# Two matmul widths for the split planes of an expert layer, an addition behind them, and two pieces of work placed elsewhere in the order

## The chip, the cores and the metric

The kernel runs on one core of a Trainium2 chip. The metric is the device time of one execution in microseconds (us). TensorE (PE; its weight loads are listed as PEld) does the matmuls, VectorE (DVE) and ScalarE (ACT) work on whole tiles, GpSimd (POOL) does small work and issues the gathers, SyncE (SP) issues the weight loads.

## The reference

The program is two transformer blocks over 256 tokens of width 1024, all in fp32. The change lies in the expert layer at the end of the first block and at the start of the second block. The expert layer is, cut to what matters:

```
q  = (xc @ w_query).reshape(C, 8, 2, 128)             # 8 heads, two halves
sc = einsum('thpd,hpnd->thpn', q, sub_keys)           # scores against 128 keys a half
... top 16 of each half, top 16 of their sums: 8 x 16 experts of 16384 for each token, softmax gates
act = gelu(einsum('cd,chkd->chk', xc, expert_down[experts]))
out = einsum('chk,chkd->cd', gates * act, expert_up[experts])
```

The second block begins with a normalisation and the projections of the normalised rows; it also needs the values of a memory of 256 rows, `mem_n @ w_kv`.

## The kernel before

**Expert layer.** The 16384 experts lie as 128 planes of 128. For the last 192 tokens (`ND = 192`) the kernel does not gather: it multiplies every plane of `expert_down` with all 192 tokens, applies gelu, multiplies with the gates (zero where an expert is not chosen), keeps the products in `slots` [128 x 128 planes x 192 tokens], and then multiplies `slots` with every plane of `expert_up`. For the first 64 tokens (`NS = 64`) it gathers the chosen rows with indirect DMAs: 64 `dot` steps (line 764, POOL fetches 128 rows, DVE multiplies and sums) and 64 `axpy` steps (line 771). These are spread over the planes (`state["k"]`, `KD`, `KU`).

**Down planes (lines 838 to 867).** The loop goes over 64 pairs of planes. One PSUM bank (`mm_tile`, a ring of four banks) takes both planes of a pair, 2 x 192 columns. The first plane of a pair is always "whole": 8 fp32 matmuls against `xf` (`whole_plane`, line 834), each of which the trace lists as two instructions. From plane `JS = 24` on the second plane of a pair is "split": the weights are loaded to `raw`, ACT rounds them to `hi` (line 61), DVE makes `lo = raw - hi` (line 62), and PE multiplies in the fp32r type: for each of 8 k-steps `hi` with `xh`, `hi` with `xl`, `lo` with `xh`, 192 columns each (`gemm_t`, lines 96 to 101). `xh` and `xl` are the two parts of the activations, two separate tiles. Before `JS` the second plane is whole too. After each pair ACT applies gelu (lines 864, 866) and DVE multiplies the tokens whose gates are ready into `slots` (line 867).

The gates of 8 tokens at a time come from `gates_of` (line 799): DVE makes one-hot tables, ACT scales one of them in 8 instructions (line 819), 16 small matmuls place the gates (line 825), DVE or ACT writes them into `slots` (lines 830, 832). 24 such groups are spread over the planes from `J0 = 34` to `J1 = 122`. What they read comes from `turns[t]` (line 742: 4 transposes on PE, copies on ACT, one DVE subtraction), called at planes 14 and 28; the tables they turn come from a long chain of top-16 searches on DVE (lines 674 to 751), which runs beside the first planes.

**Up planes (lines 899 to 927).** For each of 128 planes ACT copies the activations into `a2` (lines 904, 905, kept in program order), DVE makes their low part (line 911), the weights are split as above, and 10 matmuls of 512 columns accumulate into four banks `acc` for the whole loop, which are all four of the `mm` ring. The last three planes are held back and done first for the first 128 tokens, then for the others; DVE adds the sums to `x_sb` (lines 924, 926) and ACT takes their squares.

**Start of the second block (lines 942 to 952).** `mem_values(0)` is a product of 4 weight chunks (48 matmuls of 512 columns, `gemm_n`, line 103) into the two `at` banks. It does not depend on the expert layer. `norm_t` then normalises `x_sb` and `rows_t` transposes it for the projections.

**What sets the order.** The instructions of each engine are put into a fixed order when the program is built, by a planner that simulates the engines: work that is ready comes by its place in the program, `split` comes with a higher priority, and an instruction marked `keep_in_program_order` is not moved past others. At run time each engine works through its list.

Of the kernel before, what the change touches and what calls it, by code (L numbers as in the profile page):

```python
# [9 lines left out]
F32 = mybir.dt.float32  # L10
F32R = mybir.dt.float32r
# [4 lines left out]
OP = mybir.AluOpType  # L16
# [3 lines left out]
P = 128  # L20
T = 256
NT = 2
D = 1024
KT = 8
EPS = 1e-6
NEG = -1e30
CH = 1024
LASTN = 3
NS = 64
ND = T - NS  # L30
# [5 lines left out]
def f32v(ap):  # L36
    return ap.bitcast(F32)
# [3 lines left out]
def layers_kernel(ctx: ExitStack, tc: tile.TileContext, a: dict, out: bass.AP, upto: str = "all"):  # L41
    nc = tc.nc
    V, S, G, PE = nc.vector, nc.scalar, nc.gpsimd, nc.tensor
# [7 lines left out]
    def mm_tile():  # L51
        return psum.tile([P, 512], F32, name="mm", tag="mm", bufs=4)
# [18 lines left out]
    def stream(src, raw=None):  # L71
        if ahead:
            return ahead.pop(0)
        if raw is None:
            raw = stream_p.tile([P, CH], F32, name="raw", tag="raw", bufs=3)
        nc.sync.dma_start(raw, src)
        own = more["at"] % (3 + more["n"]) < 3
        more["at"] += 1
        pool, b = (stream_p, 3) if own else (more["pool"], more["n"])
        hi = pool.tile([P, CH], F32R, name="hi", tag="hi", bufs=b)  # L80
        lo = pool.tile([P, CH], F32R, name="lo", tag="lo", bufs=b)
        with tc.high_priority():
            split(raw, hi, lo)
        return hi, lo
# [11 lines left out]
    def gemm_t(o, xh, xl, w, kts=KT):  # L96
        for k in range(kts):
            hi, lo = w[0][:, k * P:(k + 1) * P], w[1][:, k * P:(k + 1) * P]
            PE.matmul(o, hi, xh[:, k, :], start=(k == 0), stop=False)  # L99
            PE.matmul(o, hi, xl[:, k, :], start=False, stop=False)  # L100
            PE.matmul(o, lo, xh[:, k, :], start=False, stop=(k == kts - 1))  # L101

    def gemm_n(xh, xl, w, s, kts=KT, steps=(), tail=None, bank=mm_tile):


        os = [bank() for _ in range(NT)]
        nch = kts // 2
        last = {nch - 1 - i: None for i in range(LASTN)}

        def mms(kp, w, t):  # L110
            hi, lo = w
            sl = slice(t * P, (t + 1) * P)
            for k2 in range(2):
                k = kp * 2 + k2
                wh, wl = hi[:, k2 * 512:(k2 + 1) * 512], lo[:, k2 * 512:(k2 + 1) * 512]
                PE.matmul(os[t], xh[:, k, sl], wh, start=(k == 0), stop=False)  # L116
                PE.matmul(os[t], xh[:, k, sl], wl, start=False, stop=False)  # L117
                PE.matmul(os[t], xl[:, k, sl], wh, start=False, stop=(k == kts - 1))  # L118

        for kp in range(nch):  # L120
            ws = stream(w[s, kp])
            if tail and kp in last:
                last[kp] = ws
            else:
                for t in range(NT):
                    mms(kp, ws, t)
            if kp < len(steps):
                for f in steps[kp]:
                    f()
        if tail:  # L130
            for t in range(NT):
                for kp in sorted(last):
                    mms(kp, last[kp], t)
                tail(t, os[t])
        return os
# [137 lines left out]
    with ExitStack() as c1:  # L273
        b1 = c1.enter_context(tc.tile_pool(name="b1", bufs=1))
        scr = c1.enter_context(tc.tile_pool(name="b1s", bufs=2))
        xh = b1.tile([P, KT, T], F32R, name="xh", tag="xh")
        xl = b1.tile([P, KT, T], F32R, name="xl", tag="xl")
# [293 lines left out]
    with ExitStack() as c2:  # L571
        pr = c2.enter_context(tc.tile_pool(name="peer", bufs=1))
        prs = c2.enter_context(tc.tile_pool(name="peers", bufs=2))
        xh = fx.tile([P, KT, T], F32R, name="fh")
        xl = fx.tile([P, KT, T], F32R, name="fl")
        xf = pr.tile([P, KT, ND], F32, name="ff", tag="ff")
        slots = pr.tile([P, P, ND], F32, name="slots")
        TG = 8
# [87 lines left out]
        turns = {}  # L666
# [132 lines left out]
        def gates_of(g, j):  # L799
# [20 lines left out]
            for part in range(0, TG, 4):  # L820
# [10 lines left out]
                if j < P:  # L831
                    S.copy(sv[:, j:], gv[:, j:])

        def whole_plane(o, w):
            for k in range(KT):
                PE.matmul(o, w[:, k * P:(k + 1) * P], xf[:, k, :], start=(k == 0), stop=(k == KT - 1))  # L836

        J0 = 34
        J1 = 122
        K0 = 12  # L840
        KD = 76
        JS = 24
        for jp in range(P // 2):
            j = 2 * jp
            if j >= J0:
                while state["g"] < min(NG, G0 - (-(NG - G0) * (j - J0 + 2) // (J1 - J0))):
                    gates_of(state["g"], j)
                    state["g"] += 1
            while state["k"] < KD * (jp - K0 + 1) // (P // 2 - K0):
                step()  # L850
            if j in (14, 28):
                turns[j // 14 - 1]()
            nt = state["g"] * TG - NS
            o = mm_tile()
            for jj in range(2):
                ot, src = o[:, jj * ND:(jj + 1) * ND], a["peer_down"][j + jj]
                if j >= JS and jj == 1:
                    gemm_t(ot, xh[:, :, NS:], xl[:, :, NS:], stream(src))
                else:
                    whole_plane(ot, stream_whole(src))  # L860
            ov = o[:, :2 * ND].rearrange("p (j t) -> p j t", j=2)
            dst = slots[:, j:j + 2, :]
            if nt < ND:
                S.activation(dst[:, :, nt:], ov[:, :, nt:], AF.Gelu)
            if nt > 0:
                S.activation(ov[:, :, :nt], ov[:, :, :nt], AF.Gelu)
                V.tensor_tensor(dst[:, :, :nt], ov[:, :, :nt], dst[:, :, :nt], op=OP.mult)
# [31 lines left out]
        for j in range(P):  # L899
            while state["k"] < min(2 * HALF, KD + -(-(2 * HALF - KD) * (j + 1) // KU)):  # L900
                step()

            a2 = prs.tile([P, 7 * NS], F32R, name="a2", tag="oh1")
            tc.keep_in_program_order(S.copy(a2[:, :ND], slots[:, j, :]))  # L904
            tc.keep_in_program_order(S.copy(a2[:, ND:T], slots[:, j, :NS]))
            raw = None
            if j % 6 > 2:

                raw = pr.tile([P, KT * ND], F32, name="raw_f", tag="ff")[:, :CH] if j % 6 == 4 else                     prs.tile([P, CH], F32, name="raw_o", tag="ohs")
            uh, ul = stream(a["peer_up"][j], raw)  # L910
            V.tensor_tensor(a2[:, T:], slots[:, j, :], f32v(a2[:, :ND]), op=OP.subtract)  # L911
            if j >= P - LASTN:
                held.append((j, (uh, ul, a2)))
            else:
                for t in range(NT):
                    ups(j, (uh, ul, a2), t)
# [22 lines left out]

        return [rows_p.tile([P, KT, T], F32R, name="rows_" + n, tag="rows_" + n) for n in "hl"]  # L940

    def mem_values(s, steps=(), bank=mm_tile):
        os = gemm_n(nh, nl, a["w_xv"], s, steps=steps, bank=bank)
        for t in range(NT):
            S.copy(v_m[:, t, s * 512:(s + 1) * 512], os[t])

    with ExitStack() as c3:
        b2 = c3.enter_context(tc.tile_pool(name="b2", bufs=1))
        scr = c3.enter_context(tc.tile_pool(name="b2s", bufs=1))
        xh, xl = rows_pair()  # L950
        mem_values(0, bank=at_tile)
        norm_t(x_sb, ss_mix, 2, xh, xl, [scr.tile([P, D], F32, name="xs%d" % t, tag="aT", bufs=2) for t in range(NT)])

        cols = load(b2, a["cols"], [P, 40], "cols")
# [433 lines left out]
```

## Time and profile before

| | |
|---|---|
| median of 3 runs | 1457.79 us (1457.25 to 1458.81) |
| profiled execution | 1459.28 us |
| its span, first to last instruction | 1457.2 us |
| PE busy | 1424.1 us (98%) |
| DVE busy | 1032.0 us (71%) |
| ACT busy | 769.4 us (53%) |
| POOL busy | 282.9 us (19%) |
| moved by DMA | 336.95 MB, mean 231 GB/s |

Busy time of PE is the union of its instructions. A matmul's duration in the list is its passage through the array; matmuls overlap, so what one costs in a row of them is the distance from its start to the start of the next. The profiled execution took 1.49 us more than the median, and 2.08 us of it lie outside the span.

### The profile page before, as it was taken

Reading aid. Unit: us, or ns where it says so; the run is one execution under the profiler, and the core shown is the slowest. Engines: PE = TensorE matmul, PEld = TensorE weight load, DVE = VectorE, ACT = ScalarE, POOL = GpSimd, SP = SyncE. Lnnn points to the kernel's source line nnn. Section 1 sums busy time; section 2 is a strip of 40 time slices with the busy share of each in tenths; the row PEclk is TensorE's granted clock in tenths of the full one; section 3 lists DMA queues with packets and bytes.
Section 4 is the critical chain, followed back from the end, with each engine's and each line's share of the span. In section 5 each row is a group of like instructions: output and inputs, shape, how many; then the busy total and the mean of one; then the engine's idle time right before and its main releaser. Section 6 shows DMA issues by size and latency. Waiting matters only on the chain. (4 is left out here: it accounts for less than half of the span.)

```text
span 1457.2 us, 24511 instructions
## 1 busy us (share of the span) xinstructions
PE 1424.1 (98%) x9144; PEld 1274.8 (87%) x9144; DVE 1032.0 (71%) x1841; ACT 769.4 (53%) x1497; POOL 282.9 (19%) x222
## 2 busy tenths in 40 slices
PE   9999999999999999899999999899999999999998
PEld 7778899999999999677777778797999989899886
DVE  7975678968878887688888876464565555566553
ACT  6565552336556552466666665484445455555442
POOL 4721000133332323333333300040101100000000
PEclk9999999999999999999999999999999999999999
DMA  7535557488898888999999976434456564455553
GB/s 270 159 109 178 190 186 238 144 317 315 300 326 314 310 313 327 363 326 324 336 330 332 330 235 213 162 130 130 133 175 196 179 193 144 146 196 189 188 188 114
DMA packets 93703, 336.95 MB, mean 231 GB/s; under 512 B 10736, under 2 KB 12656, under 8 KB 92816
## 3 DMA queue, kind: packets, MB, share of 16 engines
q1 hardware_dynamic: 73376, 259.79, 52.9%
q0 software_dynamic: 19344, 73.41, 14.0%
q10 hardware_dynamic: 864, 2.19, 0.4%
q8 instruction: 72, 1.18, 0.3%
q14 instruction: 47, 0.39, 0.1%
HBM read 331.15 MB, written 4.19 MB: 230 GB/s over the span
## 5 line engine op out<-in xcount | busy, mean ns | idle before, releaser
L62 DVE TENSOR_TENSOR lo<-raw,hi 128x1024 fp32r<-128x1024 f32 x345 | 424.6, 1232 | 263.2 <-ACT hi L61 258.1
L61 ACT CAST hi<-raw 128x1024 fp32r<-128x1024 f32 x345 | 361.7, 1049 | 433.5 <-PE mm L100 163.6
L836 PE MATMUL mm<-ff,whole 128*128 128x192 f32 x1216 | 209.1, 328 | 0.0
L99 PE MATMUL mm<-rows_h,hi 128*128 128x256 f32 x736 | 204.8, 283 | 2.5 <-ACT qT_x L1226 1.1
L100 PE MATMUL mm<-rows_l,hi 128*128 128x256 f32 x736 | 205.9, 281 | 0.7 <-DVE rows_l L199 0.7
L101 PE MATMUL mm<-rows_h,lo 128*128 128x256 f32 x736 | 205.4, 281 | 1.0 <-DVE lo L62 1.0
L836 PEld LDWEIGHTS mm<-ff,whole 128*128 128x128 f32 x1216 | 196.3, 190 | 0.0
L99 PE MATMUL mm<-fh,hi 128*128 128x192 f32 (+1 forms) x544 | 155.4, 289 | 0.7 <-ACT hi L61 0.5
L101 PE MATMUL mm<-fh,lo 128*128 128x192 f32 (+1 forms) x544 | 150.2, 277 | 2.3 <-DVE lo L62 2.3
L100 PE MATMUL mm<-fl,hi 128*128 128x192 f32 (+1 forms) x544 | 151.1, 279 | 0.0
L99 PEld LDWEIGHTS mm<-rows_h,hi 128*128 128x128 f32 x736 | 137.9, 190 | 3.9 <-ACT hi L61 1.4
L100 PEld LDWEIGHTS mm<-rows_l,hi 128*128 128x128 f32 x736 | 139.1, 189 | 1.6 <-DVE rows_l L199 1.0
L101 PEld LDWEIGHTS mm<-rows_h,lo 128*128 128x128 f32 x736 | 139.1, 189 | 1.6 <-DVE lo L62 1.6
L760 POOL DMA_INDIRECT fetched<-in_down_rows,picks x64 | 82.6, 1290 | 287.8 <-DVE fetched L766 152.0
L760 POOL DMA_INDIRECT fetched<-in_peer_up,picks x64 | 98.0, 1531 | 202.0 <-DVE sums L776 183.9
L891 PE MATMUL mm<-hi,a 128*128 128x512 f32 x256 | 101.8, 398 | 6.6 <-DVE a L911 6.6
L101 PEld LDWEIGHTS mm<-fh,lo 128*128 128x128 f32 x544 | 104.6, 192 | 2.5 <-DVE lo L62 2.5
L99 PEld LDWEIGHTS mm<-fh,hi 128*128 128x128 f32 x544 | 103.9, 192 | 1.1 <-ACT hi L61 1.0
L100 PEld LDWEIGHTS mm<-fl,hi 128*128 128x128 f32 x544 | 104.6, 192 | 0.1
L894 PE MATMUL mm<-hi,a 128*128 128x512 f32 x256 | 101.7, 397 | 0.7 <-ACT a L904 0.7
L895 PE MATMUL mm<-lo,a 128*128 128x512 f32 x256 | 101.7, 397 | 0.0
L892 PE MATMUL mm<-lo,a 128*128 128x512 f32 x256 | 101.7, 397 | 0.0
(379 smaller groups left out, 2827.0 us busy)
## 6 DMA issues: line engine op xcount, KB each, us to landing
whole<-in_peer_down SPq DMA_DIRECT2D x76, 512.0 KB, 4.8
raw<-in_peer_up SPq DMA_DIRECT2D x65, 512.0 KB, 6.2
raw<-in_peer_down SPq DMA_DIRECT2D x52, 512.0 KB, 5.7
raw<-in_w_in_2t SPq DMA_DIRECT2D x52, 512.0 KB, 3.5
raw_o<-in_peer_up SPq DMA_DIRECT2D x42, 512.0 KB, 6.2
raw<-in_w_up SPq DMA_DIRECT2D x32, 512.0 KB, 3.6
raw<-in_w_down SPq DMA_DIRECT2D x32, 512.0 KB, 3.5
raw<-in_w_in SPq DMA_DIRECT2D x24, 512.0 KB, 4.4
```

What stands on the lines that cost most here:

```text
L61: S.copy(hi, src)
L62: V.tensor_tensor(lo, src, f32v(hi), op=OP.subtract)
L99: PE.matmul(o, hi, xh[:, k, :], start=(k == 0), stop=False)
L100: PE.matmul(o, hi, xl[:, k, :], start=False, stop=False)
L101: PE.matmul(o, lo, xh[:, k, :], start=False, stop=(k == kts - 1))
L760: G.indirect_dma_start(out=r, out_offset=None, in_=tables[table], in_offset=bass.IndirectOffsetOnAxis(ap=picks[:, k:k + 1], axis=0))
L836: PE.matmul(o, w[:, k * P:(k + 1) * P], xf[:, k, :], start=(k == 0), stop=(k == KT - 1))
L891: PE.matmul(acc[0][hf], both, uh[:, ds], start=first, stop=False)
L892: PE.matmul(acc[0][hf], both, ul[:, ds], start=False, stop=last)
L894: PE.matmul(acc[1][hf], high, uh[:, ds], start=first, stop=False)
L895: PE.matmul(acc[1][hf], high, ul[:, ds], start=False, stop=False)
```

## The change

The two parts of the activations become one tile (`xhl`), so that both stand beside each other for each k-step. A split plane now goes to a bank of its own: for each k-step `hi` is multiplied with 384 columns (high and low part of 192 tokens), `lo` with 192, in 16 instructions for 24; the low half of the result is then copied by ACT to `part` and added by DVE to the high half, into the pair's bank. `JS` goes from 24 to 32, `J0` from 34 to 36, and the turns from planes 14 and 28 to 18 and 32. The `a2` of the first two up planes is made before the last pair of down planes. In the `mem_values(0)` call the first matmul of each token tile is kept in program order. (One long line is also written as four.)

```diff
-    def gemm_n(xh, xl, w, s, kts=KT, steps=(), tail=None, bank=mm_tile):
+    def gemm_n(xh, xl, w, s, kts=KT, steps=(), tail=None, bank=mm_tile, behind=False):
...
-                PE.matmul(os[t], xh[:, k, sl], wh, start=(k == 0), stop=False)
+                m = PE.matmul(os[t], xh[:, k, sl], wh, start=(k == 0), stop=False)
+                if behind and k == 0:
+                    tc.keep_in_program_order(m)
...
-        xh = fx.tile([P, KT, T], F32R, name="fh")
-        xl = fx.tile([P, KT, T], F32R, name="fl")
+        xhl = fx.tile([P, KT, 2, T], F32R, name="fhl")
+        xh, xl = xhl[:, :, 0, :], xhl[:, :, 1, :]
...
+        def split_plane(o, w):
+            o2 = o[:, :2 * ND].rearrange("p (s t) -> p s t", s=2)
+            for k in range(KT):
+                hi, lo = w[0][:, k * P:(k + 1) * P], w[1][:, k * P:(k + 1) * P]
+                if k < KT - 1:
+                    PE.matmul(o2, hi, xhl[:, k, :, NS:], start=(k == 0), stop=False)
+                PE.matmul(o[:, :ND], lo, xh[:, k, NS:], start=False, stop=False)
+                if k == KT - 1:
+                    PE.matmul(o2, hi, xhl[:, k, :, NS:], start=False, stop=True)
...
+        def parts_of(j):
+            a2 = prs.tile([P, 7 * NS], F32R, name="a2", tag="oh1")
+            tc.keep_in_program_order(S.copy(a2[:, :ND], slots[:, j, :]))
+            tc.keep_in_program_order(S.copy(a2[:, ND:T], slots[:, j, :NS]))
+            return a2
+
+        def low_parts(a2, j):
+            V.tensor_tensor(a2[:, T:], slots[:, j, :], f32v(a2[:, :ND]), op=OP.subtract)
+            return a2
+
+        parts = []
-        J0 = 34
+        J0 = 36
...
-        JS = 24
+        JS = 32
...
-            if j in (14, 28):
-                turns[j // 14 - 1]()
+            if j in (18, 32):
+                turns[j // 32]()
+            if jp == P // 2 - 1:
+                parts.extend(low_parts(parts_of(j), j) for j in range(2))
...
                 if j >= JS and jj == 1:
-                    gemm_t(ot, xh[:, :, NS:], xl[:, :, NS:], stream(src))
+                    o1 = mm_tile()
+                    split_plane(o1, stream(src))
+                    part = prs.tile([P, ND], F32, name="part", tag="part")
+                    S.copy(part, o1[:, ND:2 * ND])
+                    V.tensor_tensor(ot, o1[:, :ND], part, op=OP.add)
...
-            a2 = prs.tile([P, 7 * NS], F32R, name="a2", tag="oh1")
-            tc.keep_in_program_order(S.copy(a2[:, :ND], slots[:, j, :]))
-            tc.keep_in_program_order(S.copy(a2[:, ND:T], slots[:, j, :NS]))
+            a2 = parts[j] if j < 2 else parts_of(j)
...
-            V.tensor_tensor(a2[:, T:], slots[:, j, :], f32v(a2[:, :ND]), op=OP.subtract)
+            if j >= 2:
+                low_parts(a2, j)
...
-    def mem_values(s, steps=(), bank=mm_tile):
-        os = gemm_n(nh, nl, a["w_xv"], s, steps=steps, bank=bank)
+    def mem_values(s, steps=(), bank=mm_tile, behind=False):
+        os = gemm_n(nh, nl, a["w_xv"], s, steps=steps, bank=bank, behind=behind)
...
-        mem_values(0, bank=at_tile)
+        mem_values(0, bank=at_tile, behind=True)
```

## Rows read from the trace of the kernel before

**Rows 1.** Windows: stretch, us; busy (x) of PE, PEld, DVE, ACT, POOL; clock, DMA share, GB/s.

```profile
222.00:592.00 370.00, 364.33 (x2864) 362.88 (x2863) 303.29 (x739) 171.14 (x422) 101.09 (x79) 1.00 0.82 292
330.00:540.00 210.00, 210.00 (x1758) 209.65 (x1757) 177.57 (x301) 118.17 (x311) 65.92 (x53) 1.00 0.88 311
510.00:540.00 30.00, 30.00 (x256) 29.91 (x256) 27.41 (x45) 16.50 (x45) 8.24 (x7) 1.00 0.86 296
...
582.00:599.00 17.00, 10.38 (x79) 10.24 (x78) 11.60 (x14) 6.24 (x11) 6.58 (x8) 0.93 0.99 362
...
599.00:604.00 5.00, 5.00 (x14) 3.92 (x15) 1.12 (x1) 0.56 (x1) 1.77 (x2) 0.56 1.05 416
...
640.00:840.00 200.00, 200.00 (x859) 157.92 (x858) 172.12 (x212) 123.95 (x256) 66.39 (x40) 1.00 0.94 330
```

**Rows 2.** Waits of PE, whole span: line <- releaser, total us, times, longest.

```profile
PE mm L891 <- DVE a L911: 6.6, 1, 6.6
PE tp L191 <- DVE xs L209: 4.1, 1, 4.1
PE mm L101 <- DVE lo L62: 3.3, 3, 2.3
PE tp L745 <- DVE slots L720: 2.9, 2, 2.2
```

**Rows 3.** Timeline of PE, one pair of planes behind a group of gates: start, us, operation.

```profile
349.91 0.23 PE L825 MATMUL at<-ohs,oh 128*128 128x128 f16 x1
...
350.84 2.81 PE L836 MATMUL mm<-ff,whole 128*128 128x192 f32 x16
353.36 0.39 PE L99 MATMUL mm<-fh,hi 128*128 128x192 f32 x1
...
353.69 0.28 PE L101 MATMUL mm<-fh,lo 128*128 128x192 f32 x1
...
356.04 0.28 PE L101 MATMUL mm<-fh,lo 128*128 128x192 f32 x1
356.15 2.13 PE L836 MATMUL mm<-ff,whole 128*128 128x192 f32 x12
```

**Rows 4.** Timeline of PE among the up planes: three matmuls of 512 columns.

```profile
892.79 0.39 PE L892 MATMUL mm<-lo,a 128*128 128x512 f32 x1
...
893.25 0.39 PE L892 MATMUL mm<-lo,a 128*128 128x512 f32 x1
```

**Rows 5.** Timeline of PE among projections of 256 columns, first and twelfth of twelve.

```profile
929.44 0.28 PE L100 MATMUL mm<-rows_l,hi 128*128 128x256 f32 x1
...
930.74 0.28 PE L101 MATMUL mm<-rows_h,lo 128*128 128x256 f32 x1
```

**Rows 6.** Timeline of ACT and DVE beside the planes: reads of 192 columns of PSUM.

```profile
449.41 0.32 ACT L864 ACTIVATE slots<-mm 128x192 f32<-128x192 f32 x1
...
453.71 0.35 DVE L867 TENSOR_TENSOR slots<-mm,slots 128x192 f32<-128x192 f32 x1
```

**Rows 7.** Timeline of DVE: the product for the pair before Rows 3's.

```profile
356.11 0.21 DVE L867 TENSOR_TENSOR slots<-mm,slots 128x48 f32<-128x48 f32 x1
```

**Rows 8.** Timeline from the last down plane to the first up plane.

```profile
594.42 1.05 ACT L61 CAST hi<-raw 128x1024 fp32r<-128x1024 f32 x1 [2.33 <-DMA raw<-in_peer_up]
...
595.37 0.47 ACT L866 ACTIVATE mm<-mm 128x384 f32<-128x384 f32 x1
...
596.64 0.55 DVE L867 TENSOR_TENSOR slots<-mm,slots 128x384 f32<-128x384 f32 x1
...
598.80 0.76 PE L891 MATMUL mm<-hi,a 128*128 128x512 f32 x1 [6.62 <-DVE a L911]
```

**Rows 9.** Timeline at the end of the up planes and the start of the second block.

```profile
900.02 0.40 PE L117 MATMUL at<-lo,nh 128*128 128x512 f32 x1
...
902.35 0.40 PE L891 MATMUL mm<-hi,a 128*128 128x512 f32 x1
...
913.01 1.04 ACT L61 CAST hi<-raw 128x1024 fp32r<-128x1024 f32 x1 [1.86 <-DMA raw<-in_w_in_2t]
```

More of the change, by code (lines that the diff above doesn't have):

```diff
@@ L901, in layers_kernel @@
                 step()
-            a2 = prs.tile([P, 7 * NS], F32R, name="a2", tag="oh1")
-            tc.keep_in_program_order(S.copy(a2[:, :ND], slots[:, j, :]))
-            tc.keep_in_program_order(S.copy(a2[:, ND:T], slots[:, j, :NS]))
+            a2 = parts[j] if j < 2 else parts_of(j)
             raw = None
             if j % 6 > 2:
-                raw = pr.tile([P, KT * ND], F32, name="raw_f", tag="ff")[:, :CH] if j % 6 == 4 else                     prs.tile([P, CH], F32, name="raw_o", tag="ohs")
+                if j % 6 == 4:
+                    raw = pr.tile([P, KT * ND], F32, name="raw_f", tag="ff")[:, :CH]
+                else:
+                    raw = prs.tile([P, CH], F32, name="raw_o", tag="ohs")
             uh, ul = stream(a["peer_up"][j], raw)
-            V.tensor_tensor(a2[:, T:], slots[:, j, :], f32v(a2[:, :ND]), op=OP.subtract)
+            if j >= 2:
+                low_parts(a2, j)
             if j >= P - LASTN:
```

## The prediction

> **What bounds the kernel now.** I read the busy shares first: PE is busy for 98% of the span, so only time of PE, or of what PE waits for, can move the end. The windows show where PE is not busy. In the stretch of the down planes, 222 to 592 us, it works for 364.33 of 370 us, and from 330 to 540 us for all 210 [rows 1]; the waits of PE name what is missing: 2.9 us behind the searches before the turns, 2.3 us (the longest of L101) behind a low part, then 6.6 us before the first up plane, and 4.1 us before the first transposes of the second block [rows 2]. So there are two kinds of gain to look for: shorter PE work in a stretch that PE fills, and four stalls. The other engines in the full stretch: DVE is busy for 177.57 of 210 us (85%), ACT for 56%, the DMA engines at a share of 0.88 [rows 1]. DVE is the one with little room.
>
> **The split planes on PE.** The starts in one pair of planes give the costs. Whole plane: 350.84 to 353.36; split plane: 353.36 to 356.15; both together 5.31 us. Between the first and the last low matmul lie 21 steps in 2.35 us: 0.112 us for a matmul of 192 columns [rows 3]. 512 columns take 0.23 us [rows 4], 256 columns 1.30 us / 11 = 0.118 [rows 5]. No row has 384 columns in this type. Both longer ones cost 0.45 to 0.46 ns a column, while 192 cost 0.58: below some 250 columns something other than columns sets the step, and the weight load in front of each matmul is what lies beside it. So I take 384 on the line between 256 and 512: 0.174 us. The ends are 0.118 and 0.23. The low matmuls stay at 0.112, since the weight loads in front of them stay.
>
> Old split plane: 24 x 0.112 = 2.69 us. New: 8 x 0.174 + 8 x 0.112 = 2.29. Saved 0.40 a plane (ends: 0.85 and -0.05), on (128 - 32) / 2 = 48 planes 19.2 us (ends 40.6 and -2.4). The four planes that become whole save 0.05 each if I halve the 5.31, at most 0.27 by the starts as they stand: 0.2 us together. PE's work falls by 19.4 us.
>
> A rule weighed here: the Trainium skill, "TensorE: Matmul & The Clock Gate", section "Back-to-back issue gap", puts a matmul at the full clock at its columns / 2.4 GHz plus 2.5 ns, 162.5 ns for 384 columns. By that the saving would be 4.4 us larger. For 512 columns it gives 216 ns where the trace has 230 [rows 4], so I stay with the line through the rows.
>
> **What the split planes add.** A copy of 192 columns on ACT, 0.32 us, and an addition on DVE, 0.35 us, by reads of the same size from PSUM [rows 6]. ACT has the room. For DVE: a pair lasts 5.31 us plus 24 groups of gates over (122 - 36) / 2 = 43 pairs at 0.93 us (349.91 to 350.84) [rows 3], 0.52 us: 5.83 us. The 210 us hold 36 pairs, so DVE works 4.93 us a pair; with the addition 5.28, against a new pair of 5.44 us: 97%. In the densest part, 510 to 540 us, it worked 27.41 of 30 us [rows 1], 5.33 a pair, with the addition 5.68: there DVE is 0.24 us a pair too slow, some 3 us over the last dozen pairs with gates.
>
> The second cost is a wait. The addition waits on DVE for the copy, the copy for the last matmul of the plane; behind the addition stand the next low part, the dots and the gates, for which PE and POOL wait. And a pair now takes two of four banks: PE may start a pair only when the pair before the last is through gelu and product, one pair time (5.4 us) after its end; before it was three. The product for the pair that ended at 349.91 [rows 3] was done at 356.32 [rows 7], 6.4 us later; with copy and addition 7.1, that is 1.7 us late. DVE's list decides how often this happens; where PE waits DVE catches up, so I count it twice: 3 us. Together new stalls of 6 us, with ends of 0 (DVE keeps up) and a whole microsecond a pair (the slower rival).
>
> DMA does not bind: 311 GB/s at a share of 0.88 become some 333 when 5.83 us become 5.44; the up planes run at 330 GB/s and 0.94 with PE busy for 200 of 200 us [rows 1]. On SP's queue four weight loads change their buffer and nothing moves past another.
>
> **The moved starts.** `JS`, `J0` and the turns come later by 8, 2 and 4 planes. What moves are 4 transposes, 4 copies and a subtraction for each turn and the first low parts, past work that does not need them. The stalls of the stretch are 370 - 364.33 = 5.67 us [rows 1], all outside 330 to 540; the searches on DVE are as long as before, and turns come 4 planes (10.5 us) later, so these waits of up to 2.2 us should close; the first split plane still meets the end of the searches. I take 4 us of gain, ends -1 (gates start later) and 5.7.
>
> **From down to up planes.** PE stands for 6.62 us until 598.80 [rows 8], and the next 5 us run at a granted 0.56 [rows 1], a mixture of the two levels (1.2 and 2.4 GHz), which is 2.2 us of work: 8.8 us. The wait is a chain: ACT waited for a load until 594.42 and cast it, then gelu at 595.37, product until 597.19, parts, low parts [rows 8]. With the first two `a2` made earlier (4 short ACT copies and 2 DVE subtractions beside the last pair, where both have room), PE can start at once; but of the four `acc` banks the third and fourth are those of the last pair, and are free only after copy, addition, gelu and product. That was 597.19 - 592.18 = 5.0 us after the last matmul, and is 5.7 with the additions. PE has 2 x 4 matmuls for the other two banks, 1.9 us. I leave 3.8 us of stall and take 5 us of gain (ends 0: the stall stays long enough to take the clock; 8.8).
>
> **Memory values.** From 900.02 to 902.35 PE runs 10 memory matmuls before the last matmuls of the up planes [rows 9]. Kept in order they come behind, where PE stands for 4.1 us [rows 2]: the sums end 2.3 us earlier, PE has 2.3 us more work beside the normalisation. Gain 2.3. Ends: 4.1 (with the clock, which falls there too), and -1.9: ACT stood 1.86 us for a load in that chain [rows 9], and the weights of these matmuls now free their buffers later, so that the loads behind them come later too.
>
> **Sum.** 19.4 + 4 - 6 + 5 + 2.3 = 24.7 us. The span goes from 1457.2 to 1432.5; with the 2.1 us around it 1434.6 for the profiled execution, which was 1.5 us above the median: 1433 us.
>
> **Rivals.** (a) *Everything is covered*: no new stalls, 5.7 from the first stalls, 8.3 and 4.1 from the two others: 19.4 + 18.1 = 37.5, 1420 us. For it: DVE's idle time (32 us in 210) is spread over the stretch [rows 1], and the addition needs 36 x 0.35 = 12.6 of it. (b) *DVE becomes the bound*: the additions find DVE at 97%, and its order makes PE wait for low parts all through the gates: 20 us of new stalls in place of 6, 1447 us. For it: 27.41 of 30 us [rows 1]. Against it: the stretch after 540 us is light. (c) *The ring of banks is too short*, the slower side: every pair waits for the product of the pair before the last. With 1 us on 46 pairs the sum is 24.7 + 6 - 46 = -15: 1473 us, more where the clock falls after such waits as it did after 6.62 us [rows 8]. It decides from 30.7 / 46 = 0.67 us a pair. For it: the 6.4 us of [rows 7]; against it: pairs without gates leave DVE time to catch up. The Trainium skill, "TensorE: Matmul & The Clock Gate", section "A second HAM failure mode: psum-queue depth-cycling", describes this: cycling through PSUM banks, TensorE idles briefly between groups of matmuls and its clock swings between its levels. The trace of before shows no such swing from 330 to 540 us (granted 1.00). (d) *The wide matmul does not do what it should*: 384 columns in two pieces cost as much as 512, 0.23 us; then -2.4 in place of 19.2, gain 3: 1455 us.
>
> **How the numbers follow.** Forecast 0.55 (its own range 1426 to 1442), (a) 0.18, (b) 0.14, (c) 0.08, (d) 0.05. The range 1418 to 1450 leaves out (c), (d) and the far side of (a) and (b). What a measurement can tell here is about 0.2%, 2.9 us: slower has (c) and half of (d), 0.11; no change 0.04 from (d) and the edge of (b); faster 0.85.
>
> **What would show it.** Steps of about 0.174 and 0.112 us in a split plane, and a first-to-last time near 2.29; a pair near 5.4 us with gates counted in. DVE above 95% busy in the middle of the planes; waits of PE for an `mm` bank (on DVE's product) or for `lo` would be (c) and (b). No stall at the turns. A first up plane within 4 us of the last down plane. Memory matmuls all behind the up planes and less than 2 us before the transposes. I am wrong if the wide matmul costs more than 0.2 us, or if PE's busy share between 330 and 540 us falls under 95%.

## The result, and the profile after

The changed kernel takes 1440.11 us (median of 4 runs, 1439.46 to 1441.13) against 1457.52 us for the kernel before beside it (4 runs): ratio 0.988, 95% interval 0.9863 to 0.9897. It is 17.4 us faster; 24.5 us were forecast (1433 us), and 1440 lies inside both ranges. The profiled executions compared below differ by a little more, 19.4 us of span (1457.2 to 1437.8), because the one of before was 1.8 us above this median and the one of after 0.5 us below its own. The kernel before took 1457.5 to 1459.3 us (medians) beside the four sets of runs reported here, so a difference between medians of two sets is good to one or two microseconds.

The windows of the changed kernel (columns as in [rows 1]):

```profile
222.00:580.80 358.80, 349.13 (x2449) 343.60 (x2447) 312.81 (x784) 178.48 (x468) 107.12 (x79) 0.99 0.85 299
330.00:540.00 210.00, 202.94 (x1486) 198.44 (x1484) 187.92 (x338) 127.49 (x353) 75.47 (x53) 0.98 0.89 313
499.00:504.00 5.00, 3.35 (x16) 3.18 (x14) 5.00 (x12) 2.77 (x10) 2.61 (x2) 0.64 0.62 191
504.00:509.00 5.00, 5.00 (x23) 5.00 (x23) 3.15 (x6) 2.28 (x6) 1.14 (x1) 0.67 0.78 252
...
502.00:542.00 40.00, 39.52 (x269) 38.60 (x268) 34.96 (x60) 23.13 (x66) 11.73 (x10) 0.93 0.83 285
```

The waits of PE from 222 to 600 us:

```profile
PE at L827 <- ACT slots L834: 3.2, 2, 2.0
PE mm L842 <- DVE mm L890: 2.4, 4, 1.6
PE tp L747 <- DVE slots L722: 2.2, 1, 2.2
PE mm L849 <- DVE mm L890: 0.8, 1, 0.8
```

Before, PE was busy for all 210 us from 330 to 540 us [rows 1]; now it stands for 210 - 202.94 = 7.06 us there, and nearly all of it is at two places: a bank for the gates (`at`, L827), and a bank of the `mm` ring that the addition (L890) has not yet freed. The 6.6 us before the first up plane and the 4.1 us before the transposes [rows 2] are gone. The 2.2 us at the first turn (L747) are still there. DVE's busy share of that stretch rose from 85% to 187.92 / 210 = 89%, and not to 97%. The stretch holds 36 additions, one in 5.8 us where a pair of 5.44 us was forecast, and DVE stands idle for 22 us of it, half of that behind casts of ACT:

```profile
DVE lo L62 <- ACT hi L61: 11.3, 9, 3.3
```

The phase points, by the starts of PE's matmuls in the two profiles:

| | before | after | difference |
|---|---|---|---|
| first whole plane | 222.26 | 222.18 | -0.1 |
| last matmul of the down planes | 591.91 | 580.56 | -11.4 |
| first up plane | 598.80 | 580.76 | -18.0 |
| last matmul of the up planes | 903.52 | 884.29 | -19.2 |
| span | 1457.16 | 1437.78 | -19.4 |

**Chain of one stall.** From the timeline of all engines, what led to PE's two longest stalls in the middle:

```profile
484.23 1.22 DVE L768 SCALAR_TENSOR_TENSOR fetched<-fetched,rows_s 128x1024 f32<-128x1024 f32 x1
...
485.71 1.21 DVE L62 TENSOR_TENSOR lo<-raw,hi 128x1024 fp32r<-128x1024 f32 x1
486.95 0.33 SPq L76 DMA_DIRECT2D raw<-in_peer_down  x1
...
495.05 1.04 ACT L61 CAST hi<-raw 128x1024 fp32r<-128x1024 f32 x1 [3.56 <-DMA raw<-in_peer_down]
496.13 1.22 DVE L62 TENSOR_TENSOR lo<-raw,hi 128x1024 fp32r<-128x1024 f32 x1 [3.32 <-ACT hi L61]
497.27 1.01 DVE L832 TENSOR_TENSOR slots<-at,slots 128x384 f32<-128x384 f32 x2
497.86 0.27 ACT L834 COPY slots<-at 128x128 f32<-128x128 f32 x1 [1.10 <-DVE slots L832]
498.17 0.22 PE L827 MATMUL at<-ohs,oh 128*128 128x128 f16 x1 [1.97 <-ACT slots L834]
498.20 1.21 DVE L768 SCALAR_TENSOR_TENSOR fetched<-fetched,rows_s 128x1024 f32<-128x1024 f32 x1
499.34 1.22 DVE L768 SCALAR_TENSOR_TENSOR fetched<-fetched,rows_s 128x1024 f32<-128x1024 f32 x1
500.49 0.36 DVE L890 TENSOR_TENSOR mm<-mm,part 128x192 f32<-128x192 f32 x1
500.90 0.69 PE L842 MATMUL mm<-fhl,hi 128*128 128x384 f32 x1 [1.65 <-DVE mm L890]
```

Read it from the end. PE waits at 500.90 for a bank; the addition that frees it stands on DVE behind two dots. PE waits at 498.17 for the `at` banks; DVE empties them (L832) at 497.27, behind a low part (L62) for which it stood idle for 3.32 us. That low part waited for ACT's cast, the cast for a load, and the load was issued at 486.95, when the low part of 485.71 had ended and freed a buffer of `raw`; that one in turn had stood on DVE behind a dot and a product, its cast done since 484.63. The load then took 8.0 us, to 494.95. So a lag of DVE (1.1 us here) and a slow load make the cast late, the late cast makes DVE idle, and after this idle time everything on DVE's list is late at once. The share of the DMA engines from 484.5 to 495 us is 0.99, for 0.89 on average:

```profile
484.50:495.00 10.50, 10.50 (x81) 10.44 (x80) 8.09 (x14) 4.93 (x16) 4.00 (x3) 1.00 0.99 353
```

The loads take longer than before in general. DMA issues of the changed kernel (KB each, median us to landing), then of the kernel before:

```profile
whole<-in_peer_down SPq DMA_DIRECT2D x80, 512.0 KB, 5.5
...
raw<-in_peer_down SPq DMA_DIRECT2D x48, 512.0 KB, 6.7
```

```profile
whole<-in_peer_down SPq DMA_DIRECT2D x76, 512.0 KB, 4.8
...
raw<-in_peer_down SPq DMA_DIRECT2D x52, 512.0 KB, 5.7
```

Slower loads alone do not make the stalls: no_add (below) has the same medians, 5.5 and 6.7 us, and hardly a stall in the middle; fewer_dots has 4.9 and 5.6, about those of before, and still 5.3 us of stalls.

After the two stalls, 2.7 us apart, the granted clock is 0.64 and then 0.67 (the windows from 499 us), a mixture of the two levels of 1.2 and 2.4 GHz. Before, it was 1.00 from 330 to 540 us [rows 1], but not in all the down planes: behind the 2.3 us for which PE waited for a low part [rows 2] it stood at the lower level for some 3 us, with steps of 0.21 us where 0.112 is usual. Kernel before:

```profile
299.20 0.35 PE L101 MATMUL mm<-fh,lo 128*128 128x192 f32 x1 [2.34 <-DVE lo L62]
...
300.00:303.00 3.00, 3.00 (x16) 3.00 (x15) 3.00 (x8) 0.00 (x0) 1.94 (x2) 0.50 0.81 313
```

### The profile page after: what moved, and what is told of

The parts are those of the page before. It is cut to its first block, busy times and chain, and to the rows that moved or that the text cites. A ratio compares the mean times of both kernels' runs of the same rounds, so it can differ in the third digit from the quotient of the medians.

```text
span 1437.8 us, 23761 instructions
## 1 busy us (share of the span) xinstructions
PE 1406.3 (98%) x8728; PEld 1253.8 (87%) x8728; DVE 1042.5 (73%) x1884; ACT 776.0 (54%) x1540; POOL 289.6 (20%) x222
## 5 line engine op out<-in xcount | busy, mean ns | idle before, releaser
L62 DVE TENSOR_TENSOR lo<-raw,hi 128x1024 fp32r<-128x1024 f32 x341 | 419.5, 1231 | 252.4 <-ACT hi L61 251.4
L849 PE MATMUL mm<-ff,whole 128*128 128x192 f32 x1280 | 217.9, 327 | 0.9 <-DVE mm L890 0.8
L849 PEld LDWEIGHTS mm<-ff,whole 128*128 128x128 f32 x1280 | 210.5, 191 | 1.6 <-DVE mm L890 1.4
L762 POOL DMA_INDIRECT fetched<-in_down_rows,picks x64 | 89.7, 1401 | 275.8 <-DVE fetched L768 123.1
L842 PE MATMUL mm<-fhl,hi 128*128 128x384 f32 x336 | 105.5, 376 | 2.8 <-DVE mm L890 2.4
L923 PE MATMUL mm<-hi,a 128*128 128x512 f32 x256 | 100.0, 395 | 0.4 <-DVE a L859 0.4
L926 PE MATMUL mm<-hi,a 128*128 128x512 f32 x256 | 97.4, 396 | 2.3 <-ACT a L854 1.4
L843 PE MATMUL mm<-fhl,lo 128*128 128x192 f32 x384 | 90.4, 256 | 0.0
L928 PE MATMUL mm<-hi,a 128*128 128x512 f32 x256 | 81.8, 395 | 0.0
L778 DVE SCALAR_TENSOR_TENSOR sums<-fetched,acts,sums 128x1024 f32<-128x1024 f32 x63 | 80.5, 1278 | 0.0
L768 DVE SCALAR_TENSOR_TENSOR fetched<-fetched,rows_s 128x1024 f32<-128x1024 f32 x64 | 76.5, 1215 | 1.8 <-DMA fetched<-in_down_rows,picks 1.8
L843 PEld LDWEIGHTS mm<-fhl,lo 128*128 128x128 f32 x384 | 73.6, 193 | 0.0
```

The lines of the kernel that those rows point to most:

```text
L62: V.tensor_tensor(lo, src, f32v(hi), op=OP.subtract)
L762: G.indirect_dma_start(out=r, out_offset=None, in_=tables[table], in_offset=bass.IndirectOffsetOnAxis(ap=picks[:, k:k + 1], axis=0))
L842: PE.matmul(o2, hi, xhl[:, k, :, NS:], start=(k == 0), stop=False)
L843: PE.matmul(o[:, :ND], lo, xh[:, k, NS:], start=False, stop=False)
L923: PE.matmul(acc[0][hf], both, uh[:, ds], start=first, stop=False)
```

## The experiments

The theory: the PE work is saved as forecast, and part of it is paid back because DVE, with the additions, falls behind in its fixed order. The rival: four banks are too few for pairs that take two. Edits are against the changed kernel unless it says otherwise. The profile's numbers are those of one execution each.

**wide_only**: the wide split plane and its addition alone; all else as before.

```diff
-        J0 = 36
+        J0 = 34
-        JS = 32
+        JS = 24
-            if j in (18, 32):
+            if j in (14, 28):
...
-            a2 = parts[j] if j < 2 else parts_of(j)
+            a2 = parts_of(j)
...
-        mem_values(0, bank=at_tile, behind=True)
+        mem_values(0, bank=at_tile)
```

> The wide split plane with its addition alone; JS, J0 and the turns as before, a2 of the first up planes and the memory values in their old places. Theory A (PE's work falls by 0.40 us a split plane, and waits for the two-bank ring give 8 to 10 us of it back): 52 x 0.40 = 20.8 less, 9 back, 1445 to 1449 us. Theory B (DVE, 97% busy with the addition, gives it back): the same total, but the first split planes now meet the searches on DVE as well, 1448 to 1452. Rival (the wide matmul alone brings little, the three moved pieces bring the gain): above 1453.

Measured: 1462.99 us (10 runs, 1455.09 to 1466.84) beside 1458.47, ratio 1.0018 (1.0001 to 1.0035): no faster than before. Both theories gave too little back; the time lies in the rival's range, though for another reason than little saved on PE. The window and waits (222 to 600 us), from the slowest of the ten runs:

```profile
330.00:540.00 210.00, 199.70 (x1447) 195.95 (x1445) 181.83 (x328) 124.07 (x339) 67.79 (x52) 0.97 0.88 306
```

```profile
PE at L827 <- ACT slots L834: 8.3, 5, 2.6
PE mm L842 <- DVE mm L887: 3.9, 3, 1.7
```

The down planes end at 598.03, 6.1 us later than before, though PE has less to do. So the wide plane by itself is worth nothing: the stalls and the slow clock behind them (0.97 on average in this window) eat all of it.

**narrow_rest**: everything but the wide plane.

```diff
-                    o1 = mm_tile()
-                    split_plane(o1, stream(src))
-                    part = prs.tile([P, ND], F32, name="part", tag="part")
-                    S.copy(part, o1[:, ND:2 * ND])
-                    V.tensor_tensor(ot, o1[:, :ND], part, op=OP.add)
+                    gemm_t(ot, xh[:, :, NS:], xl[:, :, NS:], stream(src))
```

> Everything of the change except the wide split plane: 24 matmuls of 192 columns again, no second bank, no copy, no addition. If the parts add up, the first stalls give 3, the way from down to up planes 5 and the memory values 3 us: 1446 to 1448 us. Rival (the wide matmul alone brings little): about 1441, as the whole change.

Measured: 1449.21 us (1447.46 to 1450.67), ratio 0.994 (0.9923 to 0.9956): 9.3 us under the 1458.47 beside it, and 1.2 us over the range expected if the parts add up. No stall in the middle:

```profile
330.00:540.00 210.00, 210.00 (x1765) 209.61 (x1765) 176.97 (x299) 118.31 (x312) 68.15 (x52) 1.00 0.88 313
```

The down planes end at 586.54, 5.4 us before those of before. On top of this kernel the wide plane is worth 1449.2 - 1440.1 = 9.1 us.

**wide_moved**: the wide plane with the moved starts, without the two reordered pieces (`a2` and the memory values as in wide_only).

```diff
-            a2 = parts[j] if j < 2 else parts_of(j)
+            a2 = parts_of(j)
...
-        mem_values(0, bank=at_tile, behind=True)
+        mem_values(0, bank=at_tile)
```

> The wide split plane with JS, J0 and the turns of the change, but a2 of the first up planes and the memory values in their old places. The two kernels that lack one of these places each took 5.2 and 3.2 us more than the change; if these add up, 1448 to 1449 us. Then the moved starts are what separates this from the wide plane alone (1455 to 1467). Rival (the wide plane alone varies by chance of the order, the starts mean little): 1455 or more.

Measured: 1446.53 us (1443.76 to 1447.77), ratio 0.991 (0.9893 to 0.9928), a little better than additive. Against wide_only the starts save 16.5 us by the medians (wide_only's runs spread over 12 us); the end of the down planes moves from 598.03 to 582.22. Without the wide plane the same starts moved that end by 5.4 us.

**wide_js32**: wide_only with `JS = 32` alone (the edit is against wide_only).

```diff
-        JS = 24
+        JS = 32
```

> As the wide plane alone, but JS = 32; J0 and the turns as before. If the eight early planes matter (split planes meet the searches on DVE): 1448 to 1451 us. If the start of the gates matters (their spacing over the pairs): 1455 to 1463, stalls of PE at the gates all through the planes as in the wide plane alone.

Measured: 1456.42 us (10 runs, 1449.15 to 1459.53), ratio 0.9974 (0.9957 to 0.999). This is the range expected if the start of the gates matters. So of the 16.5 us some 6.6 come with `JS` and 9.9 with `J0` and the turns, if taken in this order; the ten runs spread over 10 us. Its stalls are again mostly at the two places: 6.0 us in five waits for an `at` bank and 4.6 in four for the addition.

**own_ring**: the split plane's bank comes from the two `tp` banks, which stand idle beside the planes but for the turns.

```diff
-                    o1 = mm_tile()
+                    o1 = tp_tile()
```

> The whole change, but the split plane's bank comes from the two banks that only the turns use here, so that a pair takes one of the four banks again. Theory A (ring of banks): the new stalls between 330 and 540 us and the slow clock behind them go, 6 to 9 us, 1431 to 1434 us. Theory B (DVE's load): no change, 1438 to 1441, with PE now waiting for low parts instead.

Measured: 1434.04 us (1432.95 to 1435.32), ratio 0.9835 (0.9818 to 0.9851), 6.1 us under the change, the intervals apart. Window and waits:

```profile
330.00:540.00 210.00, 206.34 (x1547) 203.49 (x1547) 193.59 (x352) 131.49 (x365) 73.37 (x56) 1.00 0.92 324
```

```profile
PE at L827 <- ACT slots L834: 2.7, 2, 2.3
```

No wait for the addition is left, the stall at the gates (2.28 us at 495.75) is still there, and no other stands close behind it: the ten microseconds after it run at a granted 1.00, where the changed kernel had 0.64 and 0.67. This is theory A's outcome; theory B had said no change. DVE's share is higher than in the changed kernel, 193.59 / 210 = 92%.

**no_add**: copy and addition are replaced by one copy of the high half; the low half is left out of the sum.

```diff
-                    part = prs.tile([P, ND], F32, name="part", tag="part")
-                    S.copy(part, o1[:, ND:2 * ND])
-                    V.tensor_tensor(ot, o1[:, :ND], part, op=OP.add)
+                    S.copy(ot, o1[:, :ND])
```

> The whole change, but ACT copies the high half of the result into the pair's bank and nothing adds the low half (it is left out of the sum): DVE loses 48 operations of 0.35 us, the ring of banks and the copy on ACT stay. Theory A (ring): 1436 to 1440 us, since the chain behind a plane is only 0.4 us shorter. Theory B (DVE's load): 1430 to 1434, DVE back near 85% between 330 and 540 us and no waits of PE there.

Measured: 1432.25 us (1430.49 to 1433.33), ratio 0.9819 (0.9802 to 0.9835).

```profile
330.00:540.00 210.00, 209.81 (x1576) 207.12 (x1574) 187.83 (x316) 133.47 (x363) 73.46 (x56) 1.00 0.94 337
```

Without the addition (0.36 us of DVE in each pair) PE is as full as before the change. The time and the absent waits are theory B's outcome, its sign was not: DVE's share is 187.83 / 210 = 89% as in the changed kernel, because the pairs now pass faster. Several things changed together here: DVE has less to do, nothing on its list waits for ACT's copy, and ACT's gelu no longer waits for the addition (40.4 us of ACT's waits from 330 to 540 us in the change); no run separates them. In the profiles the down planes end 8.3 us earlier in own_ring (572.22) and 11.2 in no_add (569.38), of the 13.0 that new stalls, the clock behind them and an unassigned rest cost the planes (7.1 + 3.2 + 2.7, below); two separate prices could not give both. Part of it is lost again behind the planes: the medians are 6.1 and 7.9 us lower.

**own_ring_no_add**: both edits (the low half again left out).

```diff
-                    o1 = mm_tile()
+                    o1 = tp_tile()
...
-                    V.tensor_tensor(ot, o1[:, :ND], part, op=OP.add)
+                    S.copy(ot, o1[:, :ND])
```

> Both at once: the split plane's bank from the banks of the turns, and no addition (ACT copies the high half, the low half is left out of the sum). If ring and addition give back separate parts of the gain (6 and 8 us): 1427 to 1429 us. If they are two ways to the same stalls, as when DVE's lag shows at whichever bank PE needs next: 1431 to 1433 us, as without the addition alone.

Measured: 1432.4 us (1428.51 to 1436.97), ratio 0.9811 (0.9789 to 0.9832), the same median as no_add, but with runs 8.5 us apart. PE is busy for 210.00 of 210 us in the middle, where no_add left only 0.19 us to gain. In this profile, of the slowest run, a wait for a load (2.21 us until 323.49) delays the planes instead. So the two savings don't add. Taken together: the waits for the addition go with either edit, so they need both the addition on DVE and the short ring. The waits at the gates' banks stay with own_ring (2.7 us for 3.2) and all but go with no_add (0.2), so the addition is behind these too, and the ring is not.

**fewer_dots**: `KD = 66` for 76, ten dots fewer beside the down planes and ten more beside the up planes.

```diff
-        KD = 76
+        KD = 66
```

> The whole change with KD = 66 for 76: ten of the steps on gathered rows move from the down planes to the up planes, 11 to 12 us of DVE work. Theory B (DVE's load in the down planes): the new stalls of 6 us and the 3 us of slow clock mostly go, 1432 to 1435 us, if the up planes bear the work (DVE there 86% to 90%). Theory A (ring of banks alone): 1438 to 1441.

Measured: 1443.9 us (1443.05 to 1447.55), ratio 0.9911 (0.9894 to 0.9927): slower than the change by 3.8 us (the runs don't overlap, the intervals just do). The expectation failed in the total. In the planes it held in part: they end 5.0 us earlier (575.61 for 580.56) and the slow steps are gone, but PE still stands for 5.32 of the 210 us (7.06 in the change), although the dots take DVE some 6 us less there; less work on DVE alone did not remove the stalls. And the up planes take 311.4 us for 303.5, 4.5 us of it in this wait (PE, from 575 to 890 us):

```profile
PE mm L923 <- DVE a L859: 4.5, 2, 3.7
```

DVE's work taken from one stretch was missed in the next.

**turn_later**: the turns at planes 20 and 34 for 18 and 32.

```diff
-            if j in (18, 32):
-                turns[j // 32]()
+            if j in (20, 34):
+                turns[j // 34]()
```

> The whole change with the turns at planes 20 and 34 for 18 and 32. The transposes of the first turn stand in PE's list behind the same matmul in both kernels, and their wait of 2.2 + 0.4 us is in both traces. If the place alone makes it: the wait goes, 1437 to 1438 us. Rival (the gates start later and crowd DVE in the middle): 1440 or more.

Measured: 1441.32 us (1437.65 to 1444.98), ratio 0.9876 (0.986 to 0.9893): no change, and the expectation that the wait goes failed. The wait has moved from the first turn's transposes (2.23 us at 272.80) into the same turn's later ones, now behind the subtraction L739:

```profile
282.55 0.90 PE L747 MATMUL tp<-ident,slots 128*128 128x128 f32 x3 [2.83 <-DVE slots L739]
```

**no_parts** and **no_behind**: one reordered piece undone in each.

```diff
-                parts.extend(low_parts(parts_of(j), j) for j in range(2))
...
-            a2 = parts[j] if j < 2 else parts_of(j)
+            a2 = parts_of(j)
```

> The whole change, but a2 of the first two up planes is made after the down planes as before. If the way from down to up planes is what brought the 5 us that the two traces show between the last down plane and the last up plane: 1444 to 1446 us, with a stall of 6 us or more before the first up plane and a slow clock behind it. Rival (the last bank bounds PE there anyway): 1440 to 1441.

Measured: 1445.33 us (1444.51 to 1447.23), ratio 0.9916 (0.99 to 0.9933): the piece is worth 5.2 us. PE at the border of down and up planes without it:

```profile
580.32 0.36 PE L845 MATMUL mm<-fhl,hi 128*128 128x384 f32 x1
586.55 0.76 PE L920 MATMUL mm<-hi,a 128*128 128x512 f32 x1 [5.86 <-DVE a L859]
...
587.53 0.63 PE L920 MATMUL mm<-hi,a 128*128 128x512 f32 x1
587.96 0.63 PE L921 MATMUL mm<-lo,a 128*128 128x512 f32 x1
```

The steps of 0.43 us behind the stall, for 0.23 [rows 4], go with a granted clock of 0.57 from 586.5 to 592 us.

```diff
-        mem_values(0, bank=at_tile, behind=True)
+        mem_values(0, bank=at_tile)
```

> The whole change, but the memory values are free to go ahead of the last up planes as before. If the order brought the 3 us that the traces show behind the last up plane: 1442 to 1444 us, with a wait of some 4 us before the transposes. Rival (ACT's wait for the load ends that chain): 1440 to 1441.

Measured: 1443.3 us (1442.45 to 1444.52), ratio 0.9899 (0.9883 to 0.9916): 3.2 us, with runs that don't overlap those of the change, and intervals that just do. The transposes wait again:

```profile
901.11 1.54 PE L193 MATMUL tp<-ident,xs 128*128 128x128 f32 x6 [3.54 <-DVE xs L211]
```

**own_ring_spread**: own_ring with the gates spread further, `J1 = 126` for 122.

```diff
-                    o1 = mm_tile()
+                    o1 = tp_tile()
...
-        J1 = 122
+        J1 = 126
```

> The change with the split plane's bank from the two banks of the turns, and J1 = 126 for 122, so that 24 groups of gates lie over 45 pairs for 43. If DVE's load per pair still sets the rest of the stalls at pairs that both have a group: 1431 to 1433 us. If the end of the gates then comes too near the up planes: 1435 or more.

Measured: 1433.11 us (1431.21 to 1435.18), ratio 0.982 (0.9804 to 0.9837), not to be told from own_ring. PE is fuller in the middle, and stands before the up planes instead:

```profile
330.00:540.00 210.00, 208.72 (x1564) 205.93 (x1563) 191.66 (x347) 129.25 (x359) 73.06 (x56) 1.00 0.91 328
```

```profile
574.38 0.47 PE L923 MATMUL mm<-hi,a 128*128 128x512 f32 x1 [3.08 <-ACT hi L61]
```

Both beat the kernel before and the change; own_ring, the smaller edit, is the version to keep.

## Why the prediction was right, and where it was not

**PE's work (19.4 forecast): right.** One pair in the changed kernel:

```profile
566.12 2.76 PE L849 MATMUL mm<-ff,whole 128*128 128x192 f32 x16
568.59 0.47 PE L842 MATMUL mm<-fhl,hi 128*128 128x384 f32 x1
568.90 0.25 PE L843 MATMUL mm<-fhl,lo 128*128 128x192 f32 x1
568.99 0.36 PE L842 MATMUL mm<-fhl,hi 128*128 128x384 f32 x1
569.18 0.25 PE L843 MATMUL mm<-fhl,lo 128*128 128x192 f32 x1
...
570.80 0.36 PE L845 MATMUL mm<-fhl,hi 128*128 128x384 f32 x1
571.00 0.33 PE L849 MATMUL mm<-ff,whole 128*128 128x192 f32 x1
```

The pair takes 571.00 - 566.12 = 4.88 us where it took 5.31 [rows 3]. By the times of undisturbed planes in the two traces, start to start (a whole plane 2.60 us in a row of whole ones, 2.485 and now 2.465 in front of a split one; a split plane 2.79 and now 2.41), that is 24 x 2.60 + 52 x 2.485 + 52 x 2.79 = 336.7 before and 32 x 2.60 + 48 x 2.465 + 48 x 2.41 = 317.2 after, 19.5 us less; there are 24 groups of gates in both. Rival (d) is out. Neither sign of being wrong came, both by little: the wide matmul takes 0.197 us, and PE is busy for 202.94 / 210 = 96.6% in the middle.

**First stalls (4 forecast): 3.1, and 1.7 of clock that was not in the sum.** They were 5.67 us and are 9.67 - 7.06 = 2.61. The wait for the low part closed, and with it went the slow steps behind it, some 3.3 us at half the clock. The first turn's wait did not close: in PE's list its transposes stand behind the same number of whole-plane matmuls as before. I had taken the plane at which they are called for the place at which they run; the planner had put them there already.

**New stalls (-6 forecast): -7.1, and -3.2 of clock that was not in the sum.** This is the term that was mis-sized. The stalls are of the kind that was forecast, a late DVE and a bank too late, though not from a DVE at 97%: at 89% it has room on average and is late in places. That 6 came near 7.1 is partly luck, since the count behind it (one late pair, taken twice) knows nothing of the starts, and in wide_only the same stretch has 210 - 199.70 = 10.3 us of stalls. Left out was what PE's clock does behind the stalls: it stands at the lower level from 500 to 507 us, which costs 3.2 us (busy time times the missing share of the clock, in windows of 1 us). The down planes take 358.4 us from first to last matmul, for 369.65 before, 11.3 less. With 19.5, 3.1 and 1.7 gained and 7.1 and 3.2 lost, 14.0 were to be had; 2.7 us remain that no run here assigns. The Trainium skill, "TensorE: Matmul & The Clock Gate", section "A second HAM failure mode: psum-queue depth-cycling", says that in a kernel that cycles through PSUM banks TensorE idles briefly between groups of matmuls, that its clock then swings between its levels, and that this costs throughput. The trace of after agrees (0.64 and 0.67). The prediction had cited this for rival (c) alone and priced the clock at nothing in the forecast.

**Independent terms: wrong.** The forecast added the starts and the wide plane as if each had a price of its own. The runs show the same starts worth 5.4 us of the planes without the wide plane and 15.8 with it, in the profiles (16.5 by the medians of the whole time): with the wide plane they also decide how often the new stalls come. Had only the wide plane been made, this sum without the starts and the reordered pieces (19.4 - 6 = 13.4 faster) would have been wrong by 16 us or more.

**Down to up planes (5): 5.0.** Up to the last up matmul the gain grows from 11.4 to 19.2 us; 2.8 of these are memory matmuls that went behind, so 5.0 remain. No_parts gives 5.2. The first up matmul follows 0.2 us behind the last down matmul, and the stall for the last pair's banks came in pieces, of which this is the longest:

```profile
587.79 0.50 PE L926 MATMUL mm<-hi,a 128*128 128x512 f32 x1 [0.74 <-ACT a L854]
```

**Memory values (2.3): 3.0** in the profiles (19.4 less 16.4), 3.2 by no_behind. Both are rough: from the last up matmul to the end, the nine kernels here with this order take between 553.5 and 555.9 us, and the changed kernel's profile is the shortest. The transposes follow the last memory matmul at once:

```profile
895.49 0.39 PE L120 MATMUL at<-hi,nl 128*128 128x512 f32 x1
895.72 1.03 PE L193 MATMUL tp<-ident,xs 128*128 128x128 f32 x8
```

Together 19.5 + 3.1 + 1.7 - 7.1 - 3.2 - 2.7 + 5.0 + 3.0 = 19.3 of span, which the profiles have as 19.4; the sum had 24.7. The agreement proves nothing by itself, since the 2.7, the 5.0 and the 3.0 are differences between the same phase points.

**Rivals.** (a) is out by the stalls that came (its sum has 8.3 us for the way to the up planes, where the paragraph on it gives 8.8 as the end). (b) and (c) were put as two mechanisms; the runs show the addition behind both kinds of stalls, and the short ring needed for one of them, at about half of the price that (b) gave (7.1 + 3.2 for 20 us). In wide_only the price is high enough to take all of the gain.

**What stays open.** Why the later starts make the stalls fewer is argued, not shown. In the profile of the change the stalls of the middle come about every 50 us (393, 446 and 498 us). That is also the time in which the spacing of the gates repeats: two groups stand 6 us apart, for some 11 elsewhere, at 418, 469 and 525 us; but the stalls do not lie there. Moving `JS` and `J0` shifts what is on DVE's list beside the gates; no run separates this from DVE simply having more time. The ten runs of wide_only spread over 12 us, so where the stalls fall also differs from run to run.

## What to carry to other kernels

When an edit shortens the engine that is full, work out how full the next engine in the loop becomes, and follow its list in order: at 89% on average it made late whatever stood behind one delayed operation, and the stall appeared elsewhere, at a PSUM bank. The busy share alone does not tell: DVE is at 89% with 7.06 us of stalls (the change), at 89% with 0.19 (no_add) and at 92% with 3.66 (own_ring). Price a new stall on TensorE with the clock behind it, and test an edit together with the spacing it needs: the wide plane alone was worth nothing here, with later starts and a bank of its own 15 us (1449.2 to 1434.0). Banks that another phase owned and did not use at the time were the cheapest slack here.

## What the runs showed of the hardware

- Alternating matmuls of 384 and 192 columns (fp32r) do not each keep their own step: 0.197 us from the wide one to the narrow one, 0.089 back, where 0.112 was read from a row of equal matmuls and 0.174 interpolated between two such rows. The sum, 0.286, is the same.
- A stall of about 2.2 us is not always followed by the lower clock, and its length does not decide. The wait at the first turn (2.2 us, shortly before 273 us) is in thirteen of the fourteen kernels here; the granted clock behind it stays at 1.00 in nine of them, the changed one among them, and is at the lower level for some 4 us in four (no_add, own_ring_no_add, wide_moved, wide_js32). First after, then no_add:

```profile
273.00:283.00 10.00, 9.62 (x60) 9.32 (x60) 10.00 (x47) 2.48 (x5) 0.00 (x0) 1.00 0.49 157
```

```profile
273.00:277.00 4.00, 4.00 (x16) 4.00 (x15) 4.00 (x24) 0.00 (x0) 0.00 (x0) 0.57 0.07 12
```

- In the change and in wide_only two stalls close together were followed by a longer slow stretch: some 7 us after 1.97 and 1.65 us in the first (2.7 us apart), and as much in the second after 1.93 and 1.40 us (the first window below), 2.55 and 0.84 us (the third), and 1.75 and 1.70 us; in no_parts, after 0.92 and 1.65 us, it was some 4 us. The second window follows a single stall there (1.49 us until 446.8):

```profile
408.00:416.00 8.00, 5.86 (x34) 5.68 (x34) 7.12 (x15) 3.96 (x13) 4.20 (x3) 0.62 0.66 196
447.00:457.00 10.00, 10.00 (x76) 9.87 (x74) 9.26 (x18) 6.93 (x19) 1.77 (x2) 1.00 0.93 318
499.00:509.00 10.00, 9.16 (x53) 8.89 (x52) 8.35 (x16) 5.02 (x15) 3.77 (x3) 0.67 0.64 202
```
